# Four heads' chunked scan in a two-layer hybrid encoder: one exponential per block, its bias summed in PSUM, and the block's parts summed by TensorE

## The chip, the core and the metric

The kernel is one program on one NeuronCore of a Trainium2 chip. The metric is the device time of one execution in microseconds (us); less is better. The engines are TensorE (PE; PEld are its weight loads), VectorE (DVE), ScalarE (ACT), GpSimd (POOL) and SyncE (SP), which issues most DMAs. The engines run each its own instruction stream in order and meet at semaphores.

## What is computed

Two layers of an encoder on 1024 tokens of width 1024. Each layer projects the input, runs four mixers side by side (A latent attention, B Hyena convolution, C windowed attention, D a bidirectional Mamba-2 scan), projects back, and ends with a gated MLP and a gated embedding. The change lies in mixer D. Cut to what matters, with `SSD_CHUNK` 128, four heads in two groups, and state size 128:

```python
def ssd_chunked(x, a, bm, cm):              # once per direction
    a_cs = jnp.cumsum(A, axis=-1)
    seg = a_cs[..., :, None] - a_cs[..., None, :]
    lmat = jnp.exp(jnp.where(tril, seg, -jnp.inf))
    cb = jnp.einsum('bctgn,bcsgn->bgcts', Cc, Bc)
    y_diag = jnp.einsum('bgcts,bgrcts,bcsgrp->bctgrp', cb, lmat, X)
    ...                                     # states of the chunks, scanned: prev
    y_off = jnp.einsum('bctgn,cbgrpn,bgrct->bctgrp', Cc, prev, jnp.exp(a_cs))
    return (y_diag + y_off).reshape(b, s, h, p)

y = y_f + y_b + dsum * xs                   # both directions and the skip term
y_d = y * jax.nn.silu(ssd_z)                # gate
```

All tensors are float32; the kernel must agree with this reference.

## The kernel before

The kernel is written with a tile framework: the code creates tiles in pools, and a scheduler sets the order of the instructions on each engine, gives the tiles their slots and places the waits. Flows are Python generators: `interleave` advances several of them by turns, `stagger` starts one block after another so that several are under way at different steps. In what follows Lnnn is a line of the kernel before.

Each layer first projects its input while the Hyena mixer runs (`proj`, `hyena`). Then comes the stage that is changed: `ssd` (mixer D), `swa` (mixer C) and `mla_keys` (the keys of mixer A) are interleaved. After it `mla` (attention A), the output projection, the MLP and the rest follow. The stage lies at about 401 to 528 us in the first layer and at about 1978 to 2104 us in the second.

In the stage, `ssd` handles 8 chunks of 128 tokens for each of two head groups g. `states(c, g)` transposes x and B of a chunk (L846, L847), multiplies x by its decay (`xd`, on DVE), and forms the chunk's state by a matmul; `prev` gets the scanned states of both directions. `output(c, g)`, called 16 times in a layer, forms a block in these steps:

- `bc`, one PSUM bank of four 128x128 quarters (two directions d, two heads h): a mask (L880), then eight small float32r matmuls that add the cumulated decay (L885).
- Four exponentials (ACT, `Lm`), one for each quarter, each with its own per-partition bias, a column of `lg` (log dt minus the cumulated decay).
- `pc`, a second bank: C times B, and C times `prev`. DVE adds the two directions of `Lm` into `wt`, multiplies `pc`'s right half by the decay into `yo`, and `wt` by C times B.
- `yo` of the two directions are added on POOL, transposed by TensorE (L906) into a third bank `py`, copied out by ACT (`yt`); `wt` is multiplied with x on TensorE into the same bank, and two DVE additions (one for each head's 64 partitions) put the sum into `res[1, g]`, the tile that held B.

When a group's blocks are done, z and x are loaded again, and two passes of 128x1024 add the skip term and multiply by the gate; then y is stored.

PSUM: the pool `ps1` has four banks (tag `ps`) that `ssd`, the keys and part of `swa` share; `ps2` has two pairs of banks (tag `pp`). SBUF: the pool `xp` has 8 slots of 8 KB a partition under the tag X, for which `ssd` takes 7 in this stage (three `xbc`, two `prev`, two `xt`) and the keys 4 (`kT`), in part from slots that `ssd` has left. The tiles named `wraw` have two slots, through which the raw weights and reloaded tensors pass. The new pool of the stage takes over the memory of the pool before it, so its first tiles wait until the last stores of the projections (`cv` to the buffer `z`) have been read out of it.

Of the kernel before, what the change touches and what calls it, by code (L numbers as in the profile page):

```python
# [10 lines left out]
F32 = mybir.dt.float32  # L11
F32R = mybir.dt.float32r
AF = mybir.ActivationFunctionType
ALU = mybir.AluOpType
# [5 lines left out]
L, T, D, FF = 2, 1024, 1024, 2816  # L20
# [34 lines left out]
def stagger(items):  # L55

    items, live = iter(items), []
    while True:
        new = next(items, None)
        if new is not None:  # L60
            live.append(new)
        if not live:
            return
        for g in list(live):
            if next(g, live) is live:
                live.remove(g)
        yield
# [7 lines left out]
class Trunk:  # L75
# [743 lines left out]
    def ssd(self, l, ss, scal, xbc, zd, yd):  # L819
        nc = self.nc  # L820
        Ah, Al, lg, w, dec, dsum, eacs = scal
        res = {}
# [5 lines left out]
        s2 = self.pool(ss, f"sq{l}", 2)  # L828
        prev, xt = [], []
        for g in range(2):  # L830
            prev.append(self.xp.tile([128, 8, 2, 128], F32, name="prev", tag="X"))
            xt.append(self.xp.tile([128, 8, 2, 128], F32, name="xt", tag="X"))
        for g in range(2):
            nc.gpsimd.memset(prev[g][:, 0, 0, :], 0.0)
            nc.gpsimd.memset(prev[g][:, 7, 1, :], 0.0)

        def jv(a, c, g, n):

            return a[:, c, :].rearrange("p (d h) -> p d h", d=2)[:, :, 2 * g:2 * g + 2].unsqueeze(3).to_broadcast([128, 2, 2, n])
# [35 lines left out]
        def output(c, g):  # L875
            cs = slice(c * 128, (c + 1) * 128)
            bc = self.one()
            bv = bc.rearrange("p (d h t) -> p d h t", d=2, h=2)
            Lm = s2.tile([128, 2, 2, 128], F32, name="Lm", bufs=5)
            nc.tensor.matmul(bv, self.identr, self.mask.unsqueeze(2).to_broadcast([128, 2, 2, 128]), start=True, stop=False)  # L880
            for d in range(2):
                for h in range(2):
                    j = d * 4 + g * 2 + h
                    for a in (Ah, Al):
                        nc.tensor.matmul(bv[:, d, h, :], a[:, c, j:j + 1].to_broadcast([128, 128]), self.tri[:, d, :],  # L885
                                         start=False, stop=a is Al and d + h == 2)
            yield
            for d in range(2):
                for h in range(2):
                    j = d * 4 + g * 2 + h  # L890
                    self.act(Lm[:, d, h, :], bv[:, d, h, :], AF.Exp, bias=lg[:, c, j:j + 1])
            yield
            pc = self.one()
            self.mm(pc[:, 0:128], [(res[1, g][:, cs], res[2, g][:, cs])])
            self.mm(pc[:, 256:512], [(res[2, g][:, cs], prev[g][:, c].rearrange("p d x -> p (d x)"))])
            wt = s2.tile([128, 2, 128], F32, name="wt", bufs=3)
            self.tt(wt, Lm[:, 0], Lm[:, 1], ALU.add)
            yield
            yo = s2.tile([128, 2, 2, 64], F32, name="yo", bufs=3)
            self.tt(yo, pc[:, 256:512].rearrange("p (d h x) -> p d h x", d=2, h=2), jv(eacs, c, g, 64), ALU.mult)  # L900
            self.tt(wt, wt, pc[:, 0:128].unsqueeze(1).to_broadcast([128, 2, 128]), ALU.mult)
            yield
            self.tt(yo[:, 0], yo[:, 0], yo[:, 1], ALU.add, nc.gpsimd)
            yield
            py = self.one()
            nc.tensor.transpose(py[:, 256:384], yo[:, 0].rearrange("p h x -> p (h x)"), self.ident)  # L906
            yield
            yt = s2.tile([128, 128], F32, name="yt", bufs=3)
            self.act(yt, py[:, 256:384])
            self.mm(py[:, 0:256], [(xt[g][:, c, 0], wt.rearrange("p h t -> p (h t)"))])  # L910
            yield
            y = res[1, g]
            for h in range(2):
                hs = slice(h * 64, h * 64 + 64)
                self.tt(y[hs, cs], py[hs, h * 128:h * 128 + 128], yt[hs], ALU.add)

        items = [(states, c, 0) for c in range(8)] + [(states, c, 1) for c in range(4)]
        for c in range(4):
            items += [(output, c, 0), (states, c + 4, 1)]
        items += [(output, c, 0) for c in range(4, 8)] + [(output, c, 1) for c in range(8)]  # L920
        yield from stagger(f(c, g) for f, c, g in items)
        for g in range(2):
            nc.sync.dma_start(res[2, g], zd[:, g, :])
            x = self.wp.tile([128, T], F32, name="wraw", tag="wraw", bufs=2)
            nc.sync.dma_start(x, xbc[0][:, g])
            self.stt(res[1, g], x, dsum[:, g:g + 1], res[1, g], ALU.mult, ALU.add)
            self.tt(res[1, g], res[1, g], res[2, g], ALU.mult, nc.gpsimd if g else nc.vector)
        yield
        for hf in range(2):
            cs = slice(hf * 512, (hf + 1) * 512)  # L930
            for g in range(2):
# [903 lines left out]
```

## Time and profile before

| | |
|---|---|
| time, median of 3 runs | 3204.69 us (3196.22 to 3207.54) |
| profiled execution, its own time | 3194.46 us |
| its span, first to last instruction | 3192.7 us |
| busy over the span | PE 2946.4 us (92%), PEld 2420.9 (76%), DVE 2440.4 (76%), ACT 1291.6 (40%), POOL 1771.2 (55%) |
| mean granted TensorE clock | 0.97 |
| share of the chain that ended last | PE 48%, DVE 22%, POOL 9%, DMA 8%, issue 8%, ACT 5% |

The shares are averages over stages with different limits; the stage of the change is some 250 us of the 3193, both layers together. TensorE's ends are modelled, so its busy time is no proof that it worked at its peak. In the chain of waits a row says how long the work that ended last was held at one engine and line. A wait in brackets behind an instruction names what ended the idle time in front of it.

### The profile page before, as it was taken

Reading aid. Unit: us, or ns where it says so; the run is one execution under the profiler, and the core shown is the slowest. Engines: PE = TensorE matmul, PEld = TensorE weight load, DVE = VectorE, ACT = ScalarE, POOL = GpSimd, SP = SyncE. Lnnn points to the kernel's source line nnn. Section 1 sums busy time; section 2 is a strip of 40 time slices with the busy share of each in tenths; the row PEclk is TensorE's granted clock in tenths of the full one; section 3 lists DMA queues with packets and bytes.
Section 4 is the critical chain, followed back from the end, with each engine's and each line's share of the span. In section 5 each row is a group of like instructions: output and inputs, shape, how many; then the busy total and the mean of one; then the engine's idle time right before and its main releaser. Section 6 shows DMA issues by size and latency. Waiting matters only on the chain.

```text
span 3192.7 us, 40546 instructions
## 1 busy us (share of the span) xinstructions
PE 2946.4 (92%) x14316; PEld 2420.9 (76%) x14316; DVE 2440.4 (76%) x3711; ACT 1291.6 (40%) x2278; POOL 1771.2 (55%) x1371
## 2 busy tenths in 40 slices
PE   6999988999899999999989998889989999999996
PEld 4887866877678777787867877768767787777785
DVE  7678786878766777889777786868786677768986
ACT  4332365743333334443342333667333333344341
POOL 5455533527555666887435463335185556679845
PEclk9999998999999999999999998999999999999998
DMA  5466523022233326523335664130322333274332
GB/s 181 152 202 213 180 85 137 16 84 86 76 99 106 102 96 225 189 93 124 114 107 159 219 215 158 53 122 17 107 73 83 99 111 99 101 257 146 106 132 89
DMA packets 153427, 400.44 MB, mean 125 GB/s; under 512 B 16578, under 2 KB 43462, under 8 KB 152968
## 3 DMA queue, kind: packets, MB, share of 16 engines
q1 hardware_dynamic: 138968, 347.18, 32.5%
q0 software_dynamic: 14256, 50.67, 5.2%
q8 instruction: 114, 1.87, 0.2%
q14 instruction: 89, 0.73, 0.1%
HBM read 294.50 MB, written 103.28 MB: 125 GB/s over the span
## 4 chain that ended last, share of the span: by engine, by line
PE 48%; DVE 22%; POOL 9%; DMA 8%; issue 8%; ACT 5%; SPq 0%; DVEq 0%; POOLq 0%; ACTq 0%
PE ps L99 17%; PE pp L99 15%; PE ps L1613 7%; DMA wraw<-in_ffn_w_gate_dram 4%; POOL H L87 2%; DVE g L90 2%; DVE u L87 2%; PE ps L942 2%; DVE w L87 2%; POOL w L87 2%; DVE H L90 2%; PE ps L1054 1%; DVE v L87 1%; ACT w L84 1%; POOL wraw L87 1%
## 5 line engine op out<-in xcount | busy, mean ns | idle before, releaser
L99 PE MATMUL pp<-x,wh 128*128 128x512 f32 x1344 | 430.0, 398 | 1.8 <-ACT wh L84 1.8
L1613 PE MATMUL ps<-part 128*128 128x512 f32 x1440 | 341.4, 393 | 14.7 <-DVE H L87 6.1
L87 POOL TENSOR_TENSOR w<-wraw,w 128x512 fp32r<-128x512 f32 x164 | 232.7, 1431 | 206.0 <-ACT w L84 205.8
L1613 PEld LDWEIGHTS ps<-part 128*128 128x128 f32 x1440 | 270.8, 189 | 78.4 <-DVE H L87 9.8
L99 PEld LDWEIGHTS pp<-x,wh 128*128 128x128 f32 x1344 | 256.1, 193 | 54.2 <-ACT wh L84 2.0
L99 PE MATMUL ps<-x,w 128*128 128x512 f32 x1056 | 261.6, 395 | 10.8 <-ACT v L84 10.8
L99 PE MATMUL pp<-x,w 128*128 128x512 f32 x1056 | 258.3, 394 | 14.1 <-DVE v L87 9.7
L99 PE MATMUL pp<-x,wl 128*128 128x512 f32 x672 | 266.8, 397 | 3.8 <-POOL wl L87 3.8
L99 PE MATMUL pp<-xq,w 128*128 128x512 f32 x1056 | 264.4, 392 | 5.8 <-DVE x L87 4.5
L84 ACT ACTIVATE w<-wraw 128x512 fp32r<-128x512 f32 x264 | 152.8, 622 | 267.6 <-DMA wraw<-in_ffn_w_up_dram 169.9
L87 POOL TENSOR_TENSOR wl<-wraw,wh 128x1024 fp32r<-128x1024 f32 (+2 forms) x61 | 153.6, 2520 | 173.6 <-ACT wh L84 119.8
L99 PEld LDWEIGHTS pp<-x,w 128*128 128x128 f32 x1056 | 196.9, 188 | 63.7 <-DVE v L87 13.8
L87 POOL TENSOR_TENSOR part<-fr,part 128x512 fp32r<-128x512 f32 x140 | 220.5, 1602 | 43.7 <-ACT part L84 43.4
L99 PEld LDWEIGHTS ps<-x,w 128*128 128x128 f32 x1056 | 199.0, 190 | 59.9 <-ACT v L84 18.0
L99 PEld LDWEIGHTS pp<-xq,w 128*128 128x128 f32 x1056 | 198.0, 188 | 51.2 <-ACT w L84 5.1
L99 PE MATMUL ps<-wo,yn 128*128 128x512 f32 x768 | 188.0, 401 | 5.5 <-DVE H L90 3.1
L87 DVE TENSOR_TENSOR part<-wr,part 128x512 fp32r<-128x512 f32 x124 | 155.5, 1278 | 39.0 <-ACT part L84 38.7
L1039 POOL TENSOR_TENSOR P<-P,smr 128x1024 f32<-128x1024 f32 x64 | 121.2, 1895 | 110.1 <-DVE smr L1038 101.2
L99 PEld LDWEIGHTS ps<-wo,yn 128*128 128x128 f32 x768 | 145.4, 193 | 39.6 <-DVE H L90 5.4
L99 PE MATMUL ps<-wh,x 128*128 128x512 f32 x512 | 158.7, 390 | 0.0
L99 PEld LDWEIGHTS pp<-x,wl 128*128 128x128 f32 x672 | 129.1, 192 | 30.6 <-POOL wl L87 4.7
L90 DVE SCALAR_TENSOR_TENSOR g<-g,pp 128x1023 f32<-128x1023 f32 x88 | 128.4, 1460 | 27.0 <-ACT g L84 25.6
(385 smaller groups left out, 7264.5 us busy)
## 6 DMA issues: line engine op xcount, KB each, us to landing
fr<-fp SPq DMA_DIRECT2D x70, 512.0 KB, 3.7
c_fwd<-in_c_fwd_dram POOLq DMA_DIRECT2D x64, 512.0 KB, 5.4
wraw<-in_ffn_w_up_dram SPq DMA_DIRECT2D x50, 512.0 KB, 3.5
fp<-u SPq DMA_DIRECT2D x100, 256.0 KB, 2.4
wraw<-in_ffn_w_gate_dram SPq DMA_DIRECT2D x44, 512.0 KB, 3.8
wraw<-in_w_in_dram SPq DMA_DIRECT2D x42, 512.0 KB, 3.7
wr<-in_ffn_w_down_dram SPq DMA_DIRECT2D x36, 512.0 KB, 4.8
c_inv<-in_c_inv_dram POOLq DMA_DIRECT2D x32, 512.0 KB, 4.8
```

The costliest lines, as they stand in the source:

```text
L84: self.nc.scalar.activation(out, in_, func, **kw)
L87: (eng or self.nc.vector).tensor_tensor(out, a, b, op=op)
L90: return self.nc.vector.scalar_tensor_tensor(out, a, s, b, op0=op0, op1=op1)
L99: ins = self.nc.tensor.matmul(out, a, b, start=i == 0, stop=i == n - 1)
L942: ins = self.nc.tensor.matmul(out[0:64] if j else out, v[:, 0, :] if j else v.rearrange("p i d -> p (i d)"), terms[i][1 + j], start=k == 0 ...
L1039: nc.gpsimd.tensor_tensor(P, P, sm.to_broadcast([128, T]), op=ALU.mult)
L1054: nc.tensor.transpose(pt[:, j * 128:(j + 1) * 128], P[:, c0:c0 + 128], self.ident)
L1613: nc.tensor.matmul(ps, u, v, start=k == 0 and (p != 1 or ch == 0), stop=k == 5 and (p != 1 or ch == last))
```

## The change

`output` keeps its steps and loses some. The four biases go into PSUM ahead of the exponential: `lg` is split into two float32r parts (`lgs`), and two matmuls of 512 columns with the identity as weights add each part, spread over the 128 columns of a quarter. One exponential of 512 columns then stands in place of four. The two directions of `yo` are no longer added and transposed: two float32 matmuls with `yo` as weights and the identity as data put both into `py` feature-major, where a matmul with a diagonal matrix `skip` (from `dsum`) has put the skip term and two matmuls of 64 weight columns add x times `wt`. One DVE multiplication with the gate `zs` evicts the block. `zs` (8th slot of X) is loaded at the stage's start; the reloads of z and x and the two passes at the end of a group are gone.

```diff
+        zs = self.xp.tile([128, 2, T], F32, name="zs", tag="X")
+        for g in range(2):
+            nc.sync.dma_start(zs[:, g], zd[:, g])
+        sk = self.pool(ss, f"sk{l}")
+        skip = sk.tile([128, 2, 128], F32, name="skip")
+        for g in range(2):
+            self.act(skip[:, g], self.ident, scale=dsum[:, g:g + 1])
+        lgs = [sk.tile([128, 8, 8], F32R, name=f"lg{i}") for i in range(2)]
+        self.split(*lgs, lg)
...
             nc.tensor.matmul(bv, self.identr, self.mask.unsqueeze(2).to_broadcast([128, 2, 2, 128]), start=True, stop=False)
+            for a in lgs:
+                nc.tensor.matmul(bv, self.identr, jv(a, c, g, 128), start=False, stop=False)
...
-            for d in range(2):
-                for h in range(2):
-                    j = d * 4 + g * 2 + h
-                    self.act(Lm[:, d, h, :], bv[:, d, h, :], AF.Exp, bias=lg[:, c, j:j + 1])
+            self.act(Lm, bv, AF.Exp)
...
-            self.tt(yo[:, 0], yo[:, 0], yo[:, 1], ALU.add, nc.gpsimd)
-            yield
-            py = self.one()
-            nc.tensor.transpose(py[:, 256:384], yo[:, 0].rearrange("p h x -> p (h x)"), self.ident)
-            yield
-            yt = s2.tile([128, 128], F32, name="yt", bufs=3)
-            self.act(yt, py[:, 256:384])
-            self.mm(py[:, 0:256], [(xt[g][:, c, 0], wt.rearrange("p h t -> p (h t)"))])
-            yield
-            y = res[1, g]
+
+            py = self.one()[:, 0:128]
+            nc.tensor.matmul(py, skip[:, g], res[0, g][:, cs], start=True, stop=False)
             for h in range(2):
                 hs = slice(h * 64, h * 64 + 64)
-                self.tt(y[hs, cs], py[hs, h * 128:h * 128 + 128], yt[hs], ALU.add)
+                nc.tensor.matmul(py[hs], xt[g][:, c, 0, hs], wt[:, h], start=False, stop=False)
+            for d in range(2):
+                nc.tensor.matmul(py, yo[:, d], self.ident, start=False, stop=d == 1)
+            yield
+            self.tt(res[1, g][:, cs], py, zs[:, g, cs], ALU.mult)
...
-        for g in range(2):
-            nc.sync.dma_start(res[2, g], zd[:, g, :])
-            x = self.wp.tile([128, T], F32, name="wraw", tag="wraw", bufs=2)
-            nc.sync.dma_start(x, xbc[0][:, g])
-            self.stt(res[1, g], x, dsum[:, g:g + 1], res[1, g], ALU.mult, ALU.add)
-            self.tt(res[1, g], res[1, g], res[2, g], ALU.mult, nc.gpsimd if g else nc.vector)
-        yield
```

The scheduler sets the engines' order anew. On TensorE, in the run of blocks of the second group, one block stood as follows before (transpose, `wt` of two neighbouring blocks, `pc`, `bc` with eight matmuls L885 of which two are shown):

```order
L906 MATMUL ps<-ident,yo 128x128
L99 MATMUL ps<-wt,xt 128x256
L99 MATMUL ps<-xbc 128x128
L99 MATMUL ps<-prev,xbc 128x256
L99 MATMUL ps<-wt,xt 128x256
L880 MATMUL ps<-mask,identr 128x512
L885 MATMUL ps<-tri,s_Ah 128x128
L885 MATMUL ps<-tri,s_Al 128x128
```

The same place now (L914 to L919 are `py`, L889 to L896 `bc`, of whose eight L896 two are shown):

```order
L914 MATMUL ps<-xbc,skip 128x128
L917 MATMUL ps<-wt,xt 64x128 x2
L919 MATMUL ps<-ident,yo 128x128 x2
L99 MATMUL ps<-xbc 128x128
L99 MATMUL ps<-prev,xbc 128x256
L889 MATMUL ps<-mask,identr 128x512
L891 MATMUL ps<-lg_3574,identr 128x512
L891 MATMUL ps<-lg_3575,identr 128x512
L896 MATMUL ps<-tri,s_Ah 128x128
L896 MATMUL ps<-tri,s_Al 128x128
```

Each block now has one group `py` of five matmuls, then `pc` of the next block, then `bc` of the one after that; before, the `bc` and `pc` of two blocks alternated with single products.

On SP at the start of the stage, before (`ab` is a table for mixer C, `sq` and `sk` its queries and keys, `xs`, `bs`, `cs` the tensors of mixer D, `wyt` C's output):

```order
L1108 DMA wraw<-sq_272 128x1024
L612 DMA z_271<-cv 128x1024
L826 DMA xbc<-xs_276 128x1024 x2
L826 DMA xbc<-bs_277 128x1024 x2
L826 DMA xbc<-cs_278 128x1024 x2
L1105 DMA wraw<-sk_273 64x1024 x2
L612 DMA z_271<-cv 128x1024
L1108 DMA wraw<-sq_272 128x1024
L1160 DMA y_268<-wyt 64x128 x2
```

and now:

```order
L612 DMA z_271<-cv 128x1024
L1107 DMA wraw<-sq_272 128x1024
L826 DMA xbc<-xs_276 128x1024 x2
L826 DMA xbc<-bs_277 128x1024 x2
L826 DMA xbc<-cs_278 128x1024 x2
L835 DMA zs<-z_271 128x1024
L1104 DMA wraw<-sk_273 64x1024 x2
L1107 DMA wraw<-sq_272 128x1024
L612 DMA z_271<-cv 128x1024
L835 DMA zs<-z_271 128x1024
L1159 DMA y_268<-wyt 64x128 x2
```

The second store of z now stands behind the first half of `zs` and behind the second `sq`.

On DVE at the same time, before (`wes`, `wmx`, `wsm` and `ws` belong to mixer C's softmax):

```order
L87 TENSOR_TENSOR wes<-pp_138,wmx 128x2
L87 TENSOR_TENSOR xd<-ps,s_w 128x256 x2
L1135 TENSOR_SCALAR wmx<-wmx 128x2 x2
L87 TENSOR_TENSOR wsm<-wsm,wes 128x2
L90 SCALAR_TENSOR_TENSOR prev<-prev,s_dec,ps 128x64 x2
L1131 ISA ws,wmx<-pp,ab,pp_138 128x384
```

and now:

```order
L1134 TENSOR_SCALAR wmx<-wmx 128x2 x2
L87 TENSOR_TENSOR wsm<-wsm,wes 128x2
L1130 ISA ws,wmx<-pp,ab,pp_138 128x384
L1130 ISA wmx 128x1
L1130 ISA ws,wmx<-pp,ab,pp_138 128x384
L1130 ISA wmx 128x1
L1141 RECIPROCAL wsm<-wsm 128x2
L87 TENSOR_TENSOR wsm<-wsm,wes 128x2
L87 TENSOR_TENSOR wes<-pp_138,wmx 128x2
L1141 RECIPROCAL wsm<-wsm 128x2
L1134 TENSOR_SCALAR wmx<-wmx 128x2
L87 TENSOR_TENSOR xd<-ps,s_w 128x256 x2
```

Work of mixer C's softmax has moved in front of the first two `xd` (two small rows of `wsm` right before them are left out).

## Rows read from the trace of the kernel before

**Rows 1.** Stretches, first layer: us, then PE, PEld, DVE, ACT, POOL busy, clock, DMA.

```profile
441.00:459.00 18.00, 18.00 (x101) 13.39 (x101) 11.40 (x42) 10.80 (x31) 5.77 (x6) 0.95 0.33 102
459.00:479.00 20.00, 17.31 (x118) 15.30 (x117) 19.59 (x74) 15.21 (x57) 10.84 (x11) 1.00 0.02 5
479.00:503.50 24.50, 22.96 (x124) 18.92 (x125) 15.77 (x42) 11.11 (x41) 6.02 (x9) 0.86 0.18 60
503.50:527.50 24.00, 23.17 (x127) 15.68 (x126) 16.97 (x50) 16.08 (x43) 6.60 (x11) 1.00 0.17 46
```

**Rows 2.** The same stretches of the second layer.

```profile
2019.00:2038.00 19.00, 19.00 (x100) 14.07 (x100) 11.25 (x41) 10.55 (x31) 5.75 (x6) 0.89 0.31 91
2038.00:2058.00 20.00, 17.32 (x119) 15.28 (x117) 19.42 (x74) 15.20 (x57) 10.92 (x11) 1.00 0.02 5
2058.00:2080.00 22.00, 19.95 (x123) 16.48 (x124) 15.64 (x42) 11.03 (x41) 6.16 (x9) 1.00 0.20 67
2080.00:2103.50 23.50, 22.67 (x124) 15.50 (x123) 16.85 (x49) 16.05 (x42) 6.05 (x11) 1.00 0.15 40
```

**Rows 3.** Chain of waits, second layer: start us, us, what.

```profile
2060.03 1.15 ACT Lm L84 x4
2061.22 1.35 PE ps L99 x6
2062.58 0.23 PE ps L880
2062.81 0.84 PE ps L885 x8
2063.79 0.79 PE ps L99 x4
2064.58 0.24 PE ps L880
2064.82 0.86 PE ps L885 x8
...
2065.96 0.89 ACT Lm L84 x3
```

**Rows 4.** TensorE in order of time: start us, us, line, out<-in; idle before in brackets.

```profile
490.67 0.60 PE L99 MATMUL ps<-prev,xbc 128*128 128x256 f32 x2
491.10 0.59 PE L99 MATMUL ps<-wt,xt 128*128 128x256 f32 x2
```

**Rows 5.** One tile's instructions: ns min/median/max, first and last start.

```profile
L84 ACT ACTIVATE Lm<-ps,s_lg x128: 347/368/395, 435.2 to 2078.4; 128x128 f32<-128x128 f32 x128
L87 DVE TENSOR_TENSOR xbc<-ps,yt x64: 272/288/297, 456.3 to 2099.4; 64x128 f32<-64x128 f32 x64
L99 PE MATMUL ps<-wpt,sV x176: 379/379/686, 425.6 to 2106.4; 128*64 128x256 f32 x176
```

**Rows 6.** Start of the stage: one stretch (as rows 1), then DVE in order of time.

```profile
400.00:410.00 10.00, 6.30 (x36) 4.59 (x34) 4.05 (x18) 5.32 (x13) 0.00 (x0) 1.00 1.01 353
410.74 0.42 DVE L87 TENSOR_TENSOR xd<-ps,s_w 128x256 f32<-128x256 f32 x1 [3.77 <-DMA wraw<-sq]
411.67 0.62 DVE L1131 CUSTOM_DVE_ANT_0 ws<-pp,ab,pp 128x384 f32<-128x384 f32 x1
1987.78 0.76 DVE L87 TENSOR_TENSOR xd<-ps,s_w 128x256 f32<-128x256 f32 x2 [4.13 <-DMA z<-cv]
```

**Rows 7.** End of the stage, both layers, in order of time.

```profile
534.59 1.15 ACT L84 ACTIVATE cn<-wraw 128x256 fp32r<-128x256 f32 x2 [4.32 <-DMA wraw<-cq]
...
2108.23 1.15 ACT L84 ACTIVATE cn<-wraw 128x256 fp32r<-128x256 f32 x2 [1.44 <-DMA wraw<-cq]
```

**Rows 8.** TensorE's wait ahead of the second group's blocks, both layers.

```profile
479.00 0.46 PE L99 MATMUL ps<-xbc 128*128 128x128 f32 x2 [1.96 <-DVE xbc L87]
2057.97 0.46 PE L99 MATMUL ps<-xbc 128*128 128x128 f32 x2 [1.95 <-DVE xbc L87]
```

More of the change, by code (lines that the diff above doesn't have):

```diff
@@ L898, in output @@
             yield
-            yo = s2.tile([128, 2, 2, 64], F32, name="yo", bufs=3)
-            self.tt(yo, pc[:, 256:512].rearrange("p (d h x) -> p d h x", d=2, h=2), jv(eacs, c, g, 64), ALU.mult)
+            yo = s2.tile([128, 2, 128], F32, name="yo", bufs=3)
+            self.tt(yo.rearrange("p d (h x) -> p d h x", h=2), pc[:, 256:512].rearrange("p (d h x) -> p d h x", d=2, h=2),
+                    jv(eacs, c, g, 64), ALU.mult)
             self.tt(wt, wt, pc[:, 0:128].unsqueeze(1).to_broadcast([128, 2, 128]), ALU.mult)
             yield
-            self.tt(yo[:, 0], yo[:, 0], yo[:, 1], ALU.add, nc.gpsimd)
-            yield
-            py = self.one()
-            nc.tensor.transpose(py[:, 256:384], yo[:, 0].rearrange("p h x -> p (h x)"), self.ident)
-            yield
-            yt = s2.tile([128, 128], F32, name="yt", bufs=3)
-            self.act(yt, py[:, 256:384])
-            self.mm(py[:, 0:256], [(xt[g][:, c, 0], wt.rearrange("p h t -> p (h t)"))])
-            yield
-            y = res[1, g]
+            py = self.one()[:, 0:128]
+            nc.tensor.matmul(py, skip[:, g], res[0, g][:, cs], start=True, stop=False)
             for h in range(2):
                 hs = slice(h * 64, h * 64 + 64)
-                self.tt(y[hs, cs], py[hs, h * 128:h * 128 + 128], yt[hs], ALU.add)
+                nc.tensor.matmul(py[hs], xt[g][:, c, 0, hs], wt[:, h], start=False, stop=False)
[3 more added lines that the diff above has]
+            self.tt(res[1, g][:, cs], py, zs[:, g, cs], ALU.mult)
         items = [(states, c, 0) for c in range(8)] + [(states, c, 1) for c in range(4)]
```

## The prediction

> **What bounds the kernel now.** I read the busy shares of the stage first, stretch by stretch, then the chain of waits through it, then the tiles that the change touches. From the first block's exponentials to the last block, 441 to 527.5 us in the first layer and 2019 to 2103.5 in the second, TensorE is busy 81.4 of 86.5 us and 78.9 of 84.5 us [rows 1, 2]. The reader is to see two things there. TensorE is nearly full in the first and the last stretch of each layer, and the only stretch in which another engine is fuller is the second one, where DVE is busy 19.59 of 20 us and TensorE 17.31. ACT and POOL are never above 76% and 55% of a stretch. The idle time that TensorE shows is 5.1 us (first layer) and 5.6 us (second).
>
> The chain of waits shows what the third stretch is made of: a run of blocks of the second head group [rows 3]. From one row of `Lm` to the next but one it takes 2060.03 to 2065.96, 5.9 us for two blocks (5.7 from the next such row on). In it TensorE works nearly all the time: 1.35 + 0.23 + 0.84 + 0.79 + 0.24 + 0.86 us stand on the chain, and most of a `wt` product and a transpose run beside the exponential. TensorE's shown idle time in this stretch is 2.05 us in 22 [rows 2], so a block costs it about 2.5 us and the chain 2.85.
>
> **The change part by part.**
>
> *TensorE, per block.* Added in `bc`: two matmuls of 512 columns with the identity as weights. The mask matmul has the same shape and weights and takes 0.23 us on the chain [rows 3], so 0.46. Their data has stride zero in a row, which no matmul data in these rows has; I take the same price. Added in `py`: the skip product and two products of `yo`, each float32, 128x128. A float32 product of 256 columns is two records, 0.43 us from start to start [rows 4]; 128 columns are half, 0.21, if the weights load behind the work ahead. Eight records of 128 columns with eight sets of weights take 0.84 us [rows 3], 0.105 each, which is the same 0.21 for two. The upper bound is from the four records in 0.79 us [rows 3], a product of 128 and one of 256 columns: 0.79 - 0.43 = 0.36. I take 0.21, since the queue is full in this run. So 3 x 0.21 = 0.64 (at most 1.08). `wt` in two halves of 64 weight columns and 128 data columns is four records of 0.105, 0.42, as the one product of 0.43 before. Removed: the transpose, about 0.23, as the other rows of that kind on the chain, and not under the 0.105 of one record of 128 columns [rows 3]. Sum: 0.46 + 0.64 + 0.42 - 0.43 - 0.23 = +0.86; with the ends, +0.86 to +1.4. I take 0.89 for loose ends. 16 blocks a layer: +14.2 us.
>
> The two halves of `wt` write to different halves of the partitions. Weights of 64 columns stand in the trace, but each of those records is as long as one of 128 (379 ns for 256 columns [rows 5]), and all of them write to the same half, so it shows nothing on neighbours in two halves. The Trainium skill, "TensorE: Matmul & The Clock Gate", Part 3 (Packing small matmuls), says that products with separate column groups run at the same time. By that rule the pair would cost 0.21 and not 0.42 a block, and the sum below would be 32 x 0.21 = 6.7 us less.
>
> *ACT, DVE and POOL, per block.* Four exponentials of 0.368 us [rows 5], 1.15 us on the chain [rows 3], become one of 512 columns. It lies between 0.368, the price of 128 columns, and 1.15, that of all four; I take 0.6, nearer to the first, since part of each instruction's price does not grow with its columns; a copy `yt` and a POOL addition go; two DVE additions of 0.288 [rows 5] become one of at most that length. At the group's end two DVE passes and the reloads go. All of this lies beside TensorE's work except in two places: the exponential in the run of blocks, and DVE in the second stretch. What it gives back is therefore bounded by TensorE's idle time, and it cannot give more than that, because TensorE's own queue is what is late next.
>
> *Sum on TensorE.* If all shown idle time is taken up, the two layers grow by 14.2 - 5.1 = 9.1 and 14.2 - 5.6 = 8.6, together +17.7 us. In the run of blocks I checked that this is possible: from the end of `py` of one block to that of the next, TensorE has `pc` and `bc` (0.65 + 0.23 + 0.46 + 0.84 = 2.2 us), in which DVE must evict and then do `yo` and `wt` (three instructions, some 1.3 us by its shown pace). So the margin is about half a microsecond, and TensorE sets the pace at 2.5 + 0.89 = 3.4 us a block against 2.85.
>
> *First DVE stall.* The first `xd` instructions wait 3.77 and 4.13 us for transfers [rows 6], since their memory still holds what the second store of z reads. In the new order about 2.5 us of softmax work (two passes of 0.62 [rows 6] and some nine small ones) stands ahead of them, a gain where DVE is full afterwards. Against it, the second store of z moves behind 512 KB of `zs`, and in the second layer, where z itself was waited for, behind 512 KB of `sq` too. At 353 GB/s [rows 6] that is 1.5 us each. Net -1.0 and +0.5: -0.5. Bounds: -5 (nothing delayed) to +4 (nothing filled).
>
> *Tail.* The attention that follows waits for the second `cq` load, which needs the slot of the query weights and so the last key product; that chain is unchanged. ACT waits 4.32 us for the load in the first layer and 1.44 in the second [rows 7]. Fewer transfers stand near it now; of the difference, 2.9 us, I credit half, -1.5 (bounds -3 and 0). One wait is new: half of the `kT` tiles now take the slots of C and of the second `prev`, which the last blocks still read, where before they took slots left early (x's tile is now needed to the end). Behind it stand the keys' second halves on ACT and DVE and one of four PSUM banks. The last `pc` comes only a few matmuls after the first key, so I price it at 0; up to 2.5 us a layer otherwise.
>
> *Clock.* Ahead of the second group's blocks TensorE is idle for 1.96 and 1.95 us [rows 8]. In the first layer the granted clock is 0.86 over the stretch behind it, part of it at 1.2 GHz, and the stretch takes 24.5 us; in the second it stays at 2.4 GHz and takes 22.0 [rows 1, 2]. With less idle time ahead of it this 2.5 us may go; I count half, -1.2.
>
> Total: 17.7 - 0.5 - 1.5 - 1.2 = **+14.5 us**. Against the profiled execution's 3194.46 that is 3209.0; the median of the runs is 10.2 us above the profiled one, so on its scale 3204.69 + 14.5 = **3219 us**.
>
> **Rivals.**
>
> *TensorE keeps its waits (slower).* Its queue is in order, and each of its waits in this stage is for a product of another engine (`xd`, `prev`, `Lm`, `wt`), not for a lack of speed there. If they stay, the added 14.2 us comes on top in each layer: 28.5 - 3.2 = +25, **3230 us**. It decides from the point where DVE delivers `wt` later than TensorE ends the 2.2 us of `pc` and `bc`, so half a microsecond of slip per block is enough. For it: DVE is full in the second stretch. Against it: DVE loses about 0.3 us a block, and the exponential is shorter.
>
> *TensorE is not as full as it looks (no change).* Records overlap (0.27 us long, 0.105 apart), so each break in the flow hides up to 0.17 us of idle time under "busy"; some 25 breaks a layer would be 4 us, an estimate. With the parallel halves above or the clock in full the sum falls to 14.5 - 8 - 6.7 = about 0, **3204 us**. For it: the busy shares are modelled. Against it: in the last stretch DVE and ACT have a third of their time free, and yet TensorE is what the chain follows.
>
> *The other engines were the bound (faster).* Then DVE's relief counts: 16 x 0.29 = 4.6 us a layer and some 3.7 of passes at the groups' ends, plus the full gains at the start and the tail (5 and 3 in all): about 25 us less, **3180 us**. It needs gaps on TensorE of 14 us a layer; 5 are shown and some 4 may be hidden.
>
> **How the numbers follow.** Chances: forecast 0.52 (its own range 3210 to 3228), waits kept 0.19, hidden slack 0.18, other engines 0.11. A difference under 0.5%, 16 us, is about what a measurement of this kernel cannot tell from none; that is 3189 to 3221. Of the forecast's share a bit over four tenths lie above 3221, with nearly all of the rival that keeps the waits: 0.39 slower. Faster is the last rival and a little of the third: 0.12. The rest is 0.49. The range reaches from 3193 (the slack rival with the start's and the tail's full gain, and half the way to the last rival) to 3236 (waits kept, the dearer float32 products in part, or the key wait).
>
> **What would show it.** In the changed profile: 10 records 0.105 us apart in `py` and 11 matmuls ahead of each exponential; a block of the second group every 3.3 to 3.5 us on TensorE, with no wait for `Lm`; TensorE's busy time in the stage up by some 14 us a layer and its idle time near zero; ACT and POOL far emptier there without effect on the end. The first `xd` should wait shorter, though its transfer lands later. Wrong would be: blocks closer than 3.0 us (price too high, or halves in parallel), repeated waits of TensorE for `wt` or `yo` (rival one), or a change outside the stage, at the attention's start, larger than 4 us a layer.

## The result and the profile after

The changed kernel takes 3222.56 us (median of 4 runs, 3219.01 to 3226.39) against 3205.6 us before: a ratio of 1.0059, with a 95% interval of 1.0035 to 1.0083. In a second set of runs it was 3221.38 against 3201.42 (1.0054, 1.0041 to 1.0068). It is about half a per cent slower; 3219 was forecast.

Where the time went is read best when the stage is cut at the same events in both kernels: the *start* (last product of the projection to the first mask matmul of a block), the *blocks* (to ACT's last write of a key), and the *tail* (to the attention's first product); each is taken from start to start of these instructions. In the rows of each kernel Lnnn is a line of that kernel. First the kernel before, the two layers one after the other. Columns: stretch, its length, busy time and instructions of PE, PEld, DVE, ACT and POOL, granted clock, DMA share, GB/s.

```profile
400.30:432.50 32.20, 24.20 (x127) 18.78 (x126) 23.48 (x101) 21.46 (x63) 8.34 (x6) 0.89 0.32 109
432.50:529.90 97.40, 88.57 (x502) 68.16 (x500) 73.72 (x225) 60.82 (x187) 35.73 (x38) 0.95 0.21 60
529.90:540.30 10.40, 5.59 (x22) 4.05 (x20) 2.30 (x8) 2.82 (x7) 4.56 (x4) 0.75 0.51 162
1976.80:2010.10 33.30, 24.52 (x126) 18.95 (x125) 23.17 (x100) 21.49 (x63) 8.63 (x7) 0.85 0.32 114
2010.10:2106.40 96.30, 86.94 (x503) 66.49 (x501) 73.46 (x225) 60.83 (x187) 35.95 (x38) 0.96 0.21 61
2106.40:2113.30 6.90, 4.54 (x22) 3.03 (x21) 2.39 (x9) 2.80 (x7) 4.50 (x4) 0.91 0.52 157
```

The same six stretches of the changed kernel:

```profile
406.40:440.90 34.50, 25.10 (x119) 18.99 (x119) 26.63 (x100) 23.83 (x66) 10.09 (x9) 0.85 0.47 152
440.90:542.50 101.60, 99.79 (x649) 79.65 (x648) 64.75 (x209) 48.82 (x122) 21.94 (x20) 1.00 0.15 41
542.50:551.80 9.30, 5.37 (x26) 3.43 (x24) 3.37 (x9) 2.78 (x7) 4.54 (x4) 0.93 0.46 143
1993.70:2028.30 34.60, 23.86 (x120) 18.23 (x119) 25.76 (x100) 24.10 (x66) 10.19 (x9) 0.85 0.50 155
2028.30:2129.80 101.50, 99.70 (x649) 79.59 (x648) 64.60 (x209) 48.74 (x122) 21.83 (x20) 1.00 0.13 41
2129.80:2139.00 9.20, 5.41 (x26) 3.46 (x24) 3.38 (x9) 2.82 (x7) 4.53 (x4) 0.93 0.48 145
```

The reader is to see three things in the blocks. TensorE was idle for 8.8 and 9.4 us of them and is now for 1.8 and 1.8. Its granted clock was 0.95 and 0.96, part of the time at 1.2 GHz, and is now 1.00. DVE, ACT and POOL are each 9 to 14 us emptier, and the blocks take longer all the same.

The run of blocks of the second group, [rows 3] before, is now one repeated row of TensorE. The chain of waits of the changed kernel there (start, us, what; `L914` skip, `L917` wt, `L919` yo, the four `L99` are `pc`, `L889` mask, `L891` bias, `L896` decays, `L1148` belongs to mixer C):

```profile
491.30 0.13 PE pp L1148
491.43 0.22 PE ps L914 x2
491.65 0.37 PE ps L917 x4
492.02 0.64 PE ps L919 x4
492.66 0.66 PE ps L99 x4
493.32 0.23 PE ps L889
493.55 0.43 PE ps L891 x2
493.98 0.84 PE ps L896 x8
494.82 0.14 PE pp L1148
```

From `L1148` to `L1148` a block takes 3.52 us, 3.39 without that transpose, and no other engine stands on the chain. DVE waits for ACT and PE now, and not TensorE for them:

```profile
495.67 0.42 DVE L87 TENSOR_TENSOR wt<-Lm 128x256 f32<-128x256 f32 x1 [1.56 <-PE ps L917]
499.19 0.42 DVE L87 TENSOR_TENSOR wt<-Lm 128x256 f32<-128x256 f32 x1 [1.55 <-ACT Lm L84]
```

### The profile page after: what moved, and what is told of

It is laid out like the page before. It is cut to its first block, busy times and chain, and to the rows that moved or that the text cites. A ratio compares the mean times of both kernels' runs of the same rounds, so it can differ in the third digit from the quotient of the medians.

```text
span 3224.6 us, 40892 instructions
## 1 busy us (share of the span) xinstructions
PE 2988.7 (93%) x14604; PEld 2459.6 (76%) x14604; DVE 2424.3 (75%) x3675; ACT 1271.5 (39%) x2156; POOL 1744.5 (54%) x1337
## 4 chain that ended last, share of the span: by engine, by line
PE 47%; DVE 20%; DMA 10%; POOL 9%; issue 8%; ACT 5%; SPq 1%; DVEq 0%; POOLq 0%; ACTq 0%
PE ps L99 17%; PE pp L99 13%; PE ps L1612 7%; DMA wraw<-in_ffn_w_gate_dram 5%; DVE g L90 2%; DVE u L87 2%; POOL H L87 2%; DVE w L87 2%; PE ps L941 2%; POOL w L87 2%; DVE H L90 1%; ACT w L84 1%; PE ps L1053 1%; DMA dec<-in_c_decay_dram 1%; POOL wraw L87 1%
## 5 line engine op out<-in xcount | busy, mean ns | idle before, releaser
L99 PE MATMUL pp<-x,wh 128*128 128x512 f32 x1344 | 430.1, 398 | 1.8 <-ACT wh L84 1.8
L99 PEld LDWEIGHTS pp<-x,wh 128*128 128x128 f32 x1344 | 256.2, 193 | 54.3 <-ACT wh L84 2.0
L99 PE MATMUL ps<-x,w 128*128 128x512 f32 x1056 | 262.5, 396 | 13.9 <-ACT v L84 13.6
L99 PE MATMUL pp<-x,w 128*128 128x512 f32 x1056 | 260.2, 396 | 15.1 <-DVE v L87 8.8
L99 PE MATMUL pp<-xq,w 128*128 128x512 f32 x1056 | 265.6, 394 | 6.4 <-DVE x L87 4.6
L99 PE MATMUL pp<-x,wl 128*128 128x512 f32 x672 | 267.0, 397 | 3.8 <-POOL wl L87 3.8
L99 PEld LDWEIGHTS pp<-x,w 128*128 128x128 f32 x1056 | 197.9, 189 | 65.8 <-DVE v L87 13.2
L99 PEld LDWEIGHTS ps<-x,w 128*128 128x128 f32 x1056 | 199.7, 190 | 62.9 <-ACT v L84 20.7
L99 PEld LDWEIGHTS pp<-xq,w 128*128 128x128 f32 x1056 | 198.6, 189 | 52.7 <-ACT w L84 5.2
L99 PE MATMUL ps<-wo,yn 128*128 128x512 f32 x768 | 190.7, 407 | 5.6 <-DVE H L90 2.7
L99 PEld LDWEIGHTS ps<-wo,yn 128*128 128x128 f32 x768 | 148.5, 197 | 39.3 <-DVE H L90 4.2
L99 PE MATMUL ps<-wh,x 128*128 128x512 f32 x512 | 158.8, 390 | 0.0
L99 PEld LDWEIGHTS pp<-x,wl 128*128 128x128 f32 x672 | 129.2, 192 | 30.6 <-POOL wl L87 4.7
```

The source lines that it names most:

```text
L99: ins = self.nc.tensor.matmul(out, a, b, start=i == 0, stop=i == n - 1)
```

## The experiments

Two theories. **A**: TensorE's own work sets the pace of the blocks, so each product counts once its idle time is used up. **B**: the chain of a block through ACT, DVE and POOL sets it, and TensorE fills waits. Apart from these, **S**: the turned transfers at the start cost time. Both layers' stretches, from the single events, are added up below (us; the views above round them to 0.1); the ratio is to the kernel before in the same set of runs, whose medians were 3200.75 (bias_only to lean), 3201.42 (after_2 to yo_one) and 3200.32 (the last three); it can differ from the quotient of the medians by some 0.1%.

| kernel | time | ratio (95%) | start | blocks | tail | stage |
|---|---|---|---|---|---|---|
| before, two profiles | | | 65.4, 64.6 | 193.8, 195.3 | 17.3, 14.1 | 276.5, 274.0 |
| changed, first profile | 3222.56 | 1.0059 | 69.1 | 203.1 | 18.4 | 290.7 |
| bias_only | 3192.70 | 0.9981 (0.9971 to 0.9992) | 65.0 | 197.8 | 15.8 | 278.7 |
| no_bias | 3195.85 | 0.9992 (0.9983 to 1.0001) | 63.4 | 192.4 | 15.8 | 271.7 |
| skip_late | 3212.64 | 1.0046 (1.0034 to 1.0058) | 73.5 | 194.2 | 16.3 | 284.0 |
| lean | 3202.55 | 1.0002 (0.9990 to 1.0014) | 84.3 | 178.2 | 13.8 | 276.3 |
| after_2 (changed again) | 3221.38 | 1.0054 (1.0041 to 1.0068) | 68.7 | 203.2 | 18.8 | 290.6 |
| bias_only_2 | 3199.09 | 0.9988 (0.9980 to 0.9996) | 65.9 | 196.2 | 16.5 | 278.5 |
| bias_twice | 3229.18 | 1.0082 (1.0069 to 1.0096) | 67.8 | 216.8 | 13.9 | 298.4 |
| yo_one | 3210.57 | 1.0029 (1.0018 to 1.0040) | 69.5 | 197.5 | 13.5 | 280.5 |
| full_a | 3194.39 | 0.9982 (0.9971 to 0.9993) | 75.1 | 179.7 | 15.9 | 270.8 |
| full_b | 3193.64 | 0.9978 (0.9965 to 0.9990) | 75.7 | 176.3 | 16.5 | 268.5 |
| lean_bias | 3209.67 | 1.0027 (1.0017 to 1.0037) | 81.3 | 186.6 | 16.1 | 284.0 |

Where the first block starts later because states stand ahead of it (skip_late, lean, full), start and blocks trade against each other, and only the last column compares. In the changed kernel two things besides the blocks can differ from layer to layer: the order of the transfers at the start, and a step of some 2 us in the tail. Both are told below; they move the stage of several runs.

**The repeats (after_2, before_2).** 

> The changed kernel once more, for a second profile and a second set of runs. If the stage's longer time is the change's own, the stages take 287 to 294 us together again (first profile 290.7; before 276.5) and the time is 14 to 20 us above before. What differs outside the stage is expected to go with the time at 1.2 GHz there (190 us in the first profile, 149 in that of before), half a microsecond for each microsecond, and to be another number this time.

 

> The kernel before, once more, for a second profile of its stages: if the first (276.5 us, 41 us of it at 1.2 GHz) stands for the kernel, 274 to 280 us with at least 30 us at the lower clock, and the first block to the last key in 95 to 98 us.

 The changed kernel's stage came out at 290.6 us, the one of before at 274.0 (expected 274 to 280): the stage is 15.4 us longer, mean against mean. before_2 took 3199.74 us in its one run. The clock in its blocks was 0.96 and 0.93, and the second layer's 99.0 us lie above the 95 to 98 expected:

```profile
438.40:534.70 96.30, 86.94 (x503) 66.43 (x501) 73.48 (x224) 60.91 (x188) 35.77 (x38) 0.96 0.21 61
2011.10:2110.10 99.00, 90.21 (x503) 69.09 (x501) 73.27 (x225) 60.86 (x187) 35.97 (x38) 0.93 0.20 59
```

One expectation failed: the time outside the stage was not another number (2933.9 and 2932.2 us; before 2916.2 and 2924.0). The first profile of before ran the stretch ahead of the stage at a granted clock of 0.98 and the three others at 0.96; TensorE's instructions outside the stage are the same in number, but for one or two. By the medians the time rose by 17.0 and 20.0 us, 2 to 5 more than the stage; no run shows where that lies.

**The bias alone (bias_only, twice).** The kernel before with this part of the change only:

```diff
+            for a in lgs:
+                nc.tensor.matmul(bv, self.identr, jv(a, c, g, 128), start=False, stop=False)
...
-                    self.act(Lm[:, d, h, :], bv[:, d, h, :], AF.Exp, bias=lg[:, c, j:j + 1])
+            self.act(Lm, bv, AF.Exp)
```

> The kernel before with one part of the change alone: the bias goes into PSUM by two products of 512 columns and one exponential of 512 columns stands in place of four. Theory A (TensorE's work sets the pace in the blocks): TensorE gets 0.43 us a block more, 13.8 us in all; less of its idle time and of its time at 1.2 GHz goes back, so both stages together get 3 to 10 us longer than the 276.5 us of before, and the whole time is 3208 to 3215 us. A block of the second head group takes 3.0 to 3.2 us on TensorE. Theory B (the chain through the exponentials sets the pace, and TensorE fills its waits): ACT's 0.55 us a block less counts, the stages get 5 to 15 us shorter, 3190 to 3200 us, and a block takes under 2.85 us.

 

> The kernel before with the bias in PSUM and one exponential, once more. Theory A (TensorE's work) in the form that the first profile left: stages 277 to 282 us, 92 to 94 us of TensorE work from the first block to the last key, a block at 2.9 us; the time within 0.2% of before. If the first result (8 us below before) is the exponential's gain, it comes again: 3190 to 3196 us and stages under 276 us.

 The stage was 278.7 and 278.5 us, 2 more than the first profile of before and 3.3 more than the mean of its two, a little under the 3 to 10 that A expected; a block took 2.92 us (mean of two neighbours), where A had said 3.0 to 3.2 and B under 2.85. The time was 0.19 and 0.12% *less* (6 and 4 us), where A had said 3208 to 3215 us. In the blocks, 13.8 us of products more became only 9.0 us more busy time (185.3 against 176.3, mean of two profiles each), since the clock fell less, and 2.4 us more length. TensorE's pause of 1.95 us ahead of the second group's blocks [rows 8] is 0.80 us here (second profile):

```profile
478.88 0.47 PE L884 MATMUL ps<-mask,identr 128*128 128x512 f32 x1 [0.80 <-DVE wt L87]
```

So alone, the products cost the blocks 2.4 us: the rest lies in time that TensorE did not use (6.6 us less idle) and in time that the lower clock had cost. That the time is below that of before, where the stage is not shorter, stays open: B foretold the time, but not the stage that should have brought it.

**The bias taken out of the changed kernel, and doubled (no_bias, bias_twice).** No_bias reverses the same lines in the changed kernel. Bias_twice adds two products with zeros:

```diff
-            for a in lgs:
+            for a in lgs + [zero, zero]:
```

> The changed kernel without the two products for the bias: four exponentials with their own bias again; all else as changed. Theory A: TensorE loses 0.43 us a block, 13.8 us in all, and the stages together get 9 to 14 us shorter than the 290.7 us of the changed kernel; a block of the second group takes 2.95 to 3.1 us instead of 3.53 with its transpose; the whole time is 3208 to 3214 us. Theory B: four exponentials of 0.37 us are back on the chain and the block stays at 3.4 us or more; the time is 3220 us or more.

 

> The changed kernel with two more products of 512 columns with zeros in each block, so TensorE's price of the bias twice. Theory A: TensorE has next to no idle time left in the blocks, so the 0.43 us a block count in full: 13.8 us, stages 301 to 308 us, a block of the second group 3.9 to 4.0 us instead of 3.53; the time 3230 to 3240 us. Rival (waits on other engines are part of the 3.53 us): under 8 us more.

 Doubled, a block took 3.88 us from mask to mask, just under A's 3.9 to 4.0. The changed kernel has 3.53 with a transpose of mixer C in it, and skip_late, whose blocks have none, 3.44. The blocks became 13.6 us longer (13.8 expected). The two pairs of products in a block of bias_twice:

```profile
508.45 0.59 PE L893 MATMUL ps<-lg,identr 128*128 128x512 f32 x2
508.88 0.59 PE L893 MATMUL ps<-zero,identr 128*128 128x512 f32 x2
509.31 0.22 PE L898 MATMUL ps<-tri,s_Ah 128*128 128x128 f32 x1
```

The tail gave 4.9 us of it back and the start 0.9, so the time rose by 7.8 only, as the stage did (298.4 - 290.6), a little under A's range and inside the rival's. Taken out, the bias gave 10.8 us in the blocks, a block took 3.01 us (2.95 to 3.1 expected), and the time fell by about 21 us (0.65% between the ratios, 1.0054 and 1.0059 to 0.9992), more than A expected: 19.0 of it are in the stage, 5.5 of these in the start and 2.8 in the tail. In the start no_bias differs in more than its edit: in its second layer the store of z (issued at 1987.53) stands ahead of the second queries (1988.61) again, as in skip_late below, and that start takes 29.6 us, while the first layer keeps the turned order and takes 33.8. A holds in the blocks; start and tail follow from other things.

**One product for yo (yo_one).** The two directions are added on POOL again:

```diff
+            self.tt(yo[:, 0], yo[:, 0], yo[:, 1], ALU.add, nc.gpsimd)
-            for d in range(2):
-                nc.tensor.matmul(py, yo[:, d], self.ident, start=False, stop=d == 1)
+            nc.tensor.matmul(py, yo[:, 0], self.ident, start=False, stop=True)
```

> The changed kernel with the two directions of yo added on POOL again and one product for them in place of two. Theory A: TensorE loses 0.2 to 0.3 us a block, 7 to 9 us in all, though the addition on POOL comes in between: stages 280 to 285 us, time 3209 to 3215 us. Theory B (the chain of a block sets the pace): POOL's addition of about 0.5 us makes the chain longer, and nothing or less is gained: 3218 us or more.

 The blocks became 5.7 us shorter, the tail 5.3, the time 10.8. In the blocks A holds again, and POOL's addition is hidden; the tail's half of the gain is the step told below, not the product. One yo product takes 0.33 us to the next row, where two took 0.55 (the changed kernel's rows stand below, with the terms of the sum):

```profile
501.16 0.49 PE L919 MATMUL ps<-ident,yo 128*128 128x128 f32 x2
501.49 0.39 PE L99 MATMUL ps<-xbc 128*128 128x128 f32 x2
```

**The start (skip_late).** In the changed kernel ACT forms `skip` ahead of all else, and the two stores of z stand turned in the queue. With `skip` formed after six steps the old order returns (it can return otherwise too: no_bias has it in one layer with `skip` formed first):

```diff
-            self.act(skip[:, g], self.ident, scale=dsum[:, g:g + 1])
...
+        items.insert(6, (diag, 0, 0))      # diag: the same two ACT instructions
```

> The changed kernel with one difference: the diagonal matrix of the skip term is formed on ACT after six steps of the scan and not ahead of the first, with which the first store and the second store of z stand in the queue as in the kernel before: the first behind the load of the first queries, the second ahead of the load of the second queries. Theory S (the turned stores cost the start): the first product with xd comes 7 to 11 us after the end of the projection (the changed kernel: 14.3 and 17.4; before: 6.7 and 11.5), and both stages together get 2 to 6 us shorter; the time is 3216 to 3221 us. Rival (the softmax work that moved ahead pays for the later start, and TensorE makes up for it in the blocks): xd comes earlier, but the end of the stage stays within 1 us a layer; 3221 to 3225 us.

 In the changed kernel, second layer, the store is queued behind the load of the second queries, lands 10.96 us after its issue, and DVE's first `xd` waits for it; SP's issues, then DVE:

```profile
1997.60 1.14 SPq L1104 DMA_DIRECT2D wraw<-sk  x2
1998.84 0.54 SPq L1107 DMA_DIRECT2D wraw<-sq  x1
1999.47 0.38 SPq L612 DMA_DIRECT2D z<-cv  x1
```

```profile
2010.52 0.76 DVE L87 TENSOR_TENSOR xd<-ps,s_w 128x256 f32<-128x256 f32 x2 [2.81 <-DMA z<-cv]
```

In skip_late the store goes out ahead of those queries, and the wait is shorter:

```profile
1987.08 1.13 SPq L1109 DMA_DIRECT2D wraw<-sk  x2
1988.55 0.33 SPq L612 DMA_DIRECT2D z<-cv  x1
1990.33 0.33 SPq L1112 DMA_DIRECT2D wraw<-sq  x1
```

```profile
1998.77 0.76 DVE L87 TENSOR_TENSOR xd<-ps,s_w 128x256 f32<-128x256 f32 x2 [1.69 <-DMA z<-cv]
```

That is 11.7 us after the start of the projection's last product instead of 16.8; TensorE's first product with `xd` comes after 10.3 and 12.3 us, where 7 to 11 were expected. The stage is 6.6 us shorter, a little over the 2 to 6 expected, 2.3 of it in the tail; the time, 3212.64, lies below the 3216 to 3221 expected, 11.9 us above before by the medians, where the changed kernel's was 17.0 and 20.0. S holds; the rival, that TensorE would make it up, does not. The 6.6 us are the worth of the whole new order: more of the states, too, now stand ahead of the first block (145 products in the first layer's start in place of 119).

**Less on TensorE (lean, lean_bias).** Lean takes the changed kernel without the bias products, with yo as in yo_one, the skip term on DVE and the gate's tile loaded later:

```diff
-            nc.tensor.matmul(py, skip[:, g], res[0, g][:, cs], start=True, stop=False)
-            self.tt(res[1, g][:, cs], py, zs[:, g, cs], ALU.mult)
+            self.stt(res[1, g][:, cs], res[0, g][:, cs], dsum[:, g:g + 1], py, ALU.mult, ALU.add)
+            self.tt(res[1, g][:, cs], res[1, g][:, cs], zs[:, g, cs], ALU.mult)
```

> What the change saves without most of what it puts on TensorE: four exponentials with their own bias, the two directions of yo added on POOL and one product for both, the skip term added by DVE when the block is evicted, then the gate; the gate's tile is loaded after twelve steps of the scan; no passes and no reloads at a group's end. A block costs TensorE within 0.15 us of before. Theory A: the stages together take 268 to 278 us (before 276.5), the time is 3196 to 3206 us. Theory B (DVE, POOL or the exponentials set the pace of a block): the second addition chain on DVE shows, the stages take over 282 us, 3210 us or more.

 

> Skip term on DVE, yo added on POOL, gate's tile loaded late, and the bias in PSUM with one exponential. Against the same without the bias products (3202.55 us; a block 2.51 us): if TensorE's columns alone count, 10 to 14 us more, 3212 to 3217 us and a block of 2.94 us. If the exponentials' relief or the clock gives part of it back, as in the kernel before with the bias alone: 3195 to 3206 us.

 A's range held for lean in stage and time: as fast as before, no faster. TensorE fills these blocks too, but in the second layer a good part of them at the lower clock:

```profile
440.80:527.40 86.60, 84.65 (x533) 65.32 (x532) 61.04 (x206) 52.22 (x160) 27.30 (x35) 0.97 0.13 38
2017.20:2108.70 91.50, 89.55 (x533) 69.31 (x532) 61.00 (x206) 52.25 (x159) 27.30 (x35) 0.91 0.12 36
```

The same instructions take 4.9 us longer at 0.91 than at 0.97. Just ahead of these blocks TensorE waits 4.27 and 4.26 us for `xd` from DVE in the two layers, and 0.95 us for `wt` in the midst of them; time at 1.2 GHz follows the first in both layers, and the second in one. With the bias on top (lean_bias) the stage was 7.7 us longer, the time 0.25% (8 us) and a block 2.95 us instead of 2.51. The time lies between the two ranges: the products cost their 0.44 us in each block of that run, and 8 of 14 us in all.

**Better than both (full_a, full_b).** Full_a is the changed kernel with no_bias and skip_late together; full_b adds yo_one. No further edit.

> The changed kernel without the bias products (four exponentials) and with the skip matrix formed late, so that the transfers at the start stand as before. If both gains are TensorE's (19 us of stage from the bias products, 6.7 from the start), they add in part: stages 264 to 272 us (before 276.5), time 3186 to 3194 us. Rival (with TensorE less full, its pauses bring time at 1.2 GHz back): stages 272 to 278 us with over 10 us at the lower clock in each, time 3195 to 3202 us.

 

> As the one before, with yo's directions added on POOL and one product: TensorE 0.3 us a block less again, at most 9 us. If TensorE's work still sets the pace: stages 258 to 266 us, time 3180 to 3190 us. If its pauses and the clock take over, as where the skip term went to DVE as well (3202.55): no gain, 3194 to 3204 us.

 Both beat the kernel before, by 0.18 and 0.22%, with intervals clear of 1. Full_b's blocks:

```profile
441.00:529.50 88.50, 86.75 (x559) 67.50 (x560) 62.43 (x204) 53.14 (x165) 26.87 (x35) 1.00 0.15 42
2015.00:2102.80 87.80, 86.54 (x559) 67.46 (x560) 61.67 (x204) 53.08 (x164) 26.78 (x35) 1.00 0.15 42
```

Full_a's stage came out as its first case said (270.8 in 264 to 272); the time, 3194.39, lies just over its 3186 to 3194. Full_b's did not: 268.5 and 3193.64 fall between its two cases, and the time is level with full_a's, nearer to the case of no gain. Of the 5.7 us that one yo product was worth in yo_one's blocks, 3.4 were left. TensorE is idle for 3.0 us in full_b's blocks (full_a: 1.1), at a granted clock of 1.00; so a part went into pauses again, none of it into the clock there.

Full_b also shows where A ends. Its block costs TensorE more than lean's (2.79 us against 2.51, the skip product), and yet its stage is 7.8 us shorter. Lean has the long waits for `xd` and `wt` and the low clock just named; full_b has no pause over 0.6 us in its blocks, and no granted clock under 1.00 there. So where TensorE pauses, another engine's work does count. Lean puts the skip term on DVE and loads the gate later, both at once; which of the two makes its pauses isn't shown.

## Why the prediction was right, and where it was not

The time, the direction and the mechanism were right: in the changed kernel's blocks TensorE is what the stage follows, the block of the second group takes 3.39 us (3.4 forecast, 2.85 before), no wait for `Lm` is left on TensorE, and the others' relief buys no more than TensorE's idle time and what the clock had cost. bias_twice, yo_one and no_bias show it from both sides, with 13.6 us more and 5.7 and 10.8 less in the blocks. Of the sum (+14.5 forecast, +15.4 measured in the stage) each term was off by 4 to 9 us. They cancelled; that the sum came within 1 us is luck. Means of two profiles each, both layers:

- **Work added on TensorE**: 28.4 us forecast, about 33 measured. Busy time in the blocks went from 176.3 to 199.4 us; the 176.3 hold some 9.8 us lost to the lower clock (one minus the clock of 0.95, 0.96, 0.96 and 0.93, times the length of each stretch, for two layers), so 199.4 - 166.5. The 33 is an estimate, as this loss is. Per block it is 1.03 and not 0.89. The bias cost 0.43 us and not 0.46. The skip product, `wt` and `yo` took 1.23 us (494.80 to 496.03) and not 1.06. TensorE in the changed kernel, by records (the second row is the latter of the first row's two):

```profile
494.80 0.39 PE L914 MATMUL ps<-xbc,skip 128*128 128x128 f32 x2
494.91 0.28 PE L914 MATMUL ps<-xbc,skip 128*128 128x128 f32 x1
495.11 0.33 PE L917 MATMUL ps<-wt,xt 128*64 128x128 f32 x2
495.27 0.28 PE L917 MATMUL ps<-wt,xt 128*64 128x128 f32 x2
495.48 0.38 PE L919 MATMUL ps<-ident,yo 128*128 128x128 f32 x1
495.69 0.39 PE L919 MATMUL ps<-ident,yo 128*128 128x128 f32 x2
496.03 0.39 PE L99 MATMUL ps<-xbc 128*128 128x128 f32 x2
```

  Full-width records follow each other after 0.11 us, as forecast. The excess stands on both sides of the halves of `wt`: 0.20 us from the last skip record to `wt`, and 0.21 from the first record of `yo` to its second, in all 32 blocks of the changed kernel. So the ten records are not evenly spaced, as I had them. Full-width, 0.11 us apart (495.69 to 496.03 for three), they would take 1.11 us, so by this estimate the halves cost a block 0.12 us more than full-width products, some 4 us in all. No run has the full-width `wt` in this place; that the halves are the cause is argued, from where the excess stands.

- **Idle time taken up**: 10.7 us forecast, 14.5 measured (18.2 to 3.7). The forecast counted from 441 us on and so left out TensorE's longest pause in the blocks, ahead of the first group's last states.
- **Clock**: -1.2 forecast, -9.8 by the same working. This is the term that was most mis-sized. I took one dip of one layer. In fact either of the two long pauses of a layer was followed by time at 1.2 GHz in some profile, and the changed kernel has neither. The longer one in the first layer of before, for `xd`, and then the only pause over a microsecond that the changed kernel has in these blocks, for another tile:

```profile
439.79 1.19 PE L99 MATMUL ps<-xd,xt 128*128 128x256 f32 x2 [3.77 <-DVE xd L87]
```

```profile
445.29 1.51 PE L99 MATMUL ps<-wpt,sV 128*64 128x256 f32 x6 [1.81 <-DVE wyt L1157]
```

- **Start**: -0.5 forecast, +3.9 measured, just inside the bounds and with the wrong sign. DVE's wait is shorter (2.81 against 4.13 us in the second layer), as forecast, but ends later. I had seen the store behind `zs` and the second queries and priced 1.5 us of transfer each. I had not seen that SP itself waits there: its issue of `sk` at 1997.60 comes only when DVE has read the first queries out of their slot (a wait of 3.6 us), with the store queued behind. The first product with `xd` comes 14.3 and 17.4 us after the projection instead of 6.7 and 11.5. The start grew by less than that; the softmax work in front, which I had credited, may be why, but no run tests it. In skip_late, with the old order back, the stage is 6.6 us shorter.
- **Tail**: -1.5 forecast, +2.9 measured (15.7 to 18.6), outside its bounds. In the changed kernel TensorE waits 1.93 us for `cn` from DVE at the attention's start, in both layers of both profiles. DVE comes to `cn` late, since its copy of mixer C's output ahead of it waits 3.1 us or more for a store, and `cn` then takes 1.2 us in place of 0.41. In yo_one, whose tail is 13.5, the copy waits half as long. The second layers of the changed kernel and of yo_one:

```profile
2133.81 0.42 DVE L1157 COPY wyt<-ps 64x256 f32<-64x256 f32 x1 [3.10 <-DMA y<-wyt]
2134.15 1.22 DVE L87 TENSOR_TENSOR cn<-wraw,cn 128x256 fp32r<-128x256 f32 x1
```

```profile
2118.72 0.42 DVE L1157 COPY wyt<-ps 64x256 f32<-64x256 f32 x1 [1.49 <-DMA y<-wyt]
2119.07 0.41 DVE L87 TENSOR_TENSOR cn<-wraw,cn 128x256 fp32r<-128x256 f32 x1
```

  Over all runs a layer's tail is 8.9 to 9.5 us where `cn` is long (10 of 28 layers) and 6.5 to 7.6 in 16 of the others. Several kernels, bias_only_2 among them, have one layer of each, so a part of every difference of tails in the table is this step and not the edit's work. Why the store lands when it does isn't shown; the slots of `kT`, which I had priced at 0, weren't tried apart.

Of the rivals, "waits kept" is out, since the idle time fell from 18.2 to 3.7 us. "Not as full as it looks" is out as a whole, with one part true: the clock came back, as it said. Its other part, the parallel halves, is true of the records and not of the time: the four records of `wt` start as two pairs, at 495.11 and 495.27, but with both sides they cost more than full-width ones (see the first term). Their weight loads, and one of `yo` behind them:

```profile
495.11 0.14 PEld L917 LDWEIGHTS ps<-wt,xt 128*64 128x64 f32 x2
495.17 0.14 PEld L917 LDWEIGHTS ps<-wt,xt 128*64 128x64 f32 x2
495.59 0.19 PEld L919 LDWEIGHTS ps<-ident,yo 128*128 128x128 f32 x1
```

The first pair's weights load only when its products start (495.11); the second pair's load 0.10 us ahead of theirs (495.27), and those of the second `yo` record 0.10 us ahead (495.69). The Trainium skill, "TensorE: Matmul & The Clock Gate", Part 3 (Packing small matmuls), has it that such products run at the same time; by that the group would cost 0.21 us, an estimate, and the trace agrees as to the pairs. The same part of the Trainium skill says that a weight load overlaps with products in flight only where its row group differs. This trace does not agree: the loads at 495.17 and 495.59 use all rows, as the products started at 495.11 and 495.48 do, which by their records are still under way.

"Other engines were the bound" is out for ACT by bias_only's stage, which did not get shorter, and for the changed kernel as a whole by its own: the others are emptier, and it is slower.

## What to carry to other kernels

When work moves to an engine, first look at how much idle time it has at that place: two products of the same shape cost 2.4 us of the blocks where TensorE had 18 us of pauses and 13.6 where it had 3.7. Time at 1.2 GHz stood behind TensorE's longer pauses, so a busier TensorE can give back a part of its added work; count both in the same stretch. And a tiny edit (two instructions of ACT in skip_late) can turn the order of transfers in a scheduled kernel: compare the DMA queue of the two kernels row by row and layer by layer, and look at what its head waits for. A run with one edit has one difference only if these rows agree.

## What was not expected of the hardware

- The clock in the blocks was 0.93 to 0.96 in four stretches of the kernel before, with pauses of 3.8 and 1.95 us in each, and 1.00 in four of the changed kernel, whose longest pause was 1.81 us. After the 1.95 us pause it fell in one layer and not in the other [rows 1, 2, 8]; in the second profile of before it was the other layer's turn (0.93 against 0.96 over the blocks). In yo_one the same pause as the changed kernel's, 1.80 us, was followed by time at 1.2 GHz in the second layer (0.98 over its blocks) and not in the first, and so was a pause of 0.95 us in lean's second layer (not in its first). So these runs show no length of pause that was always harmless, and the changed kernel's 1.00 may be in part luck.
- Products with 64 weight columns in two halves of the partitions start as pairs and take 0.37 us for four records, where four full ones in a row take 0.44; but 0.09 and 0.10 us more stand in front of them and behind the next record, so that nothing is gained.
